# The first MLP's second product by Strassen's scheme with 256 moving columns, and product 3 deferred in the last chunk

## The chip, the core and the metric

The kernel runs on one core of a Trainium2 chip. A core has TensorE (matrix products into PSUM, 8 banks of 128 x 512 fp32), VectorE, ScalarE and GpSimd (POOL), and DMA engines fed by queues, here those of SP and POOL. The engines run side by side and wait for each other by semaphores. The metric is the device time of one execution in microseconds, the median of several.

## The reference

A two-layer encoder on 512 tokens of width 1024, in fp32. Layer 0 mixes by retention (4 heads) and by windowed attention (8 heads), layer 1 by axial-rope attention (8 heads). After each mixer comes an MLP with 4096 features:

```python
x = x + y                                      # y: the mixer's output
h = rms_norm(x, norm_mlp[layer])
x = x + jnp.square(jax.nn.relu(h @ w_mlp_up[layer])) @ w_mlp_down[layer]
```

Here `h` is 512 x 1024, `w_mlp_up` 1024 x 4096 and `w_mlp_down` 4096 x 1024. The text calls `h @ w_mlp_up` the first product and the one with `w_mlp_down` the second.

## The kernel before

**Three matmuls for one.** fp32 operands are split into a high part and a low rest, both of type fp32r (ScalarE casts, VectorE subtracts; `split`, L314 to L321). A product of two tiles is three matmuls, high x high, high x low and low x high (`mm3`, L326, L328, L327). Each has its own 128x128 weight load (PEld).

**Weights.** One stream, `w_stream`, loads 256 x 512 pieces (512 KB) on SP's queue into the blocks of `raws` (L459), and splits each into one of four pairs `wparts` (`cut`, L536 on ScalarE and L538 on VectorE). A piece of the plan is split when a pair comes free, so the splits run at most four pieces ahead of TensorE. `raws` holds 2 blocks until the odd layer's attention is over.

**The order.** All instructions are put in order by a planner written in the kernel: tasks ask for engines, slots and events, costs are estimated (`vec`, `act`, `pe`), and at each step the operation with the earliest estimated start goes next, with a class (EVAC first, then ATT, AUX, LOAD, GEMM) to break ties. The order on each engine is fixed by this; the chip then runs each engine's queue in order.

**First MLP** (`mlp`). Two halves of 2048 features. For each, four column chunks of the first product, then two of the second, all as plain products with the weights stationary and 512 tokens moving, so the result stands transposed (features on partitions). The second product is added to `xT` (L1223), and the next layer's input is formed from each finished tile (`after`: L316, L321).

**Second MLP** (`last_mlp`). Four chunks q of 1024 features. Each takes two column chunks of the first product, 2q and 2q+1, and a second product by Strassen's scheme in Winograd's form: the activations are cut in two token halves and two feature halves, the weights in two feature halves and two column halves (quarters), and 7 products of sums of these stand for 8. The sums of activations are formed by `rest` and `rest2` (L1325), those of weights by `sums` and `t1` (L481, L491, L499, L505; the subtraction of one quarter is done by an accumulating load on POOL's queue, L467). Products 1, 6 and 7 add up in one pair of banks, 5 and 3 in another; `add` takes them from PSUM into `acc_o` (L1398). The order is

```python
PRODUCTS = (2, 1, 4, 6, 5, 7, 3)
...
if pr == 4 and q < 3:
    yield from up(2 * q + 2, ...)      # a chunk of the first product
```

so that in chunks 0 to 2 a chunk of the first product, 96 matmuls, lies between product 4 and product 6, and in the last chunk nothing does. Here the activations are stationary and 512 columns of weights move. The stream has 9 blocks then, and 2 more (`xs`) for sums: five lent by gates and probabilities (`sh0` to `sh4`), the rest by `xT`.

**Axial tables.** `ax_tables` loads the tables for layer 1's rope when retention has ended (L1474, L1479, L307), long before they are read.

Of the kernel before, what the change touches and what calls it, by code (L numbers as in the profile page):

```python
# [17 lines left out]
P = 128  # L18
S = 512
D = 1024  # L20
# [173 lines left out]
FIXED = [0.065, 0.075]  # L194
# [10 lines left out]
def pe(n):  # L205
    return ("P", 3 * (n / 2400 + 0.0135))
# [16 lines left out]
def hybrid_encoder(ctx: ExitStack, tc: tile.TileContext, a, out):  # L223
# [10 lines left out]
    kvp = ctx.enter_context(tc.tile_pool(name="kvp", bufs=4))  # L234
# [5 lines left out]
    FIXED[:] = 0.065, 0.075  # L240
# [10 lines left out]
    raws = slots("raw", 2, (P, 2, 512), F32)  # L251
    wparts = pairs("w", 4, (P, 2, 512))
    bigs = pairs("big", 4, (P, 4, 512))
    def shared(i, dt):
        return cst.tile([P, 2, 512], dt, tag=f"sh{i}", name=f"sh{i}")

    gs = [shared(i, F32) for i in range(2)]
    pts = [shared(i, F32R) for i in range(2, 5)]
    probs_t = Slots(W, [(t[:, 0, :], t[:, 1, :]) for t in pts])
# [3 lines left out]
    xT2 = [cst.tile([P, 2, 512], F32, tag=f"xT{k}", name=f"xT{k}") for k in range(KD // 2)]  # L263
    xT = [xT2[k // 2][:, k % 2, :] for k in range(KD)]
    rB = cst.tile([P, 512], F32, name="rB")

    def kv_pair():
        both = kvp.tile([P, 2, 512], F32R, tag="kv", name="kv")
        return both[:, 0, :], both[:, 1, :]
# [103 lines left out]

    def plan_mlp(l):
        p_ = []
        for hf in range(2):
            for c in range(4):
                p_ += w_parts(f"up{l}", 0, D, hf * 2048 + c * 512)
            for c in range(2):
                p_ += w_parts(f"down{l}", hf * 2048, (hf + 1) * 2048, c * 512)  # L380
        return p_

    plan += plan_mlp(0)
    for c0 in (1024, 0, 512):
        plan += w_parts("w_in_odd", 0, D, c0)
    for r0 in (0, 512):
        for c0 in (0, 512):
            plan += w_parts("w_out_odd", r0, r0 + 512, c0)


    PRODUCTS = (2, 1, 4, 6, 5, 7, 3)
    chunk_at = {}
    loads_of = [ap for _, ap in plan]

    def plan_w(parts):
        plan.extend(parts)
        loads_of.extend(ap for _, ap in parts)

    unit_load = list(range(len(plan)))
    at_product = {}  # L400

    def quarter(q, r, c, h):
        r0 = q * 1024 + (1 - r) * 512 + h * 256
        return a["down1"][r0:r0 + 256, c * 512:c * 512 + 512]

    def plan_up(g, between=()):
        between = list(between)
        for part in w_parts("up1", 0, D, g * 512):
            for at in between[:1]:
                chunk_at[at] = len(loads_of)  # L410
                loads_of.append(quarter(*at))
            del between[:1]
            unit_load.append(len(loads_of))
            plan_w([part])
        for at in between:
            chunk_at[at] = len(loads_of)
            loads_of.append(quarter(*at))

    def plan_products(q, prs):
        for pr in prs:  # L420
            for h in range(2):
                at_product[q, pr, h] = len(plan)
                plan.append((("down1", q, pr, h), None))
                unit_load.append(None)

    plan_up(0)
    for q in range(4):
        plan_up(2 * q + 1, [(q, r, c, h) for r, c in ((0, 1), (0, 0), (1, 0)) for h in range(2)])
        plan_products(q, PRODUCTS[:3])
        last_two = [(q, 1, 1, h) for h in range(2)]  # L430
        if q < 3:
            plan_up(2 * q + 2)
        for at in last_two:
            chunk_at[at] = len(loads_of)
            loads_of.append(quarter(*at))
        plan_products(q, PRODUCTS[3:])

# [121 lines left out]
    def gemm(name, r0, r1, c0, lhs, natural, evac, cls=EVAC, bk=None, halves=False):  # L559
# [6 lines left out]
        for k0 in range(first, nk, step):  # L566
# [6 lines left out]
            for b in range(4):  # L573
                bs = slice(b * P, (b + 1) * P)
                if halves and b == 3:
                    for i, cs in enumerate((slice(0, 256), slice(256, 512))):
                        if k0 == 0:
                            halved.append((yield gbanks))
# [1168 lines left out]
```

## Time and profile before

| | |
|---|---|
| median of 3 runs | 1251.6 us (1251.45 to 1254.9) |
| the profiled execution: time, span | 1252.68 us, 1250.8 us |
| TensorE busy | 1235.5 us, 5736 matmuls |
| VectorE, ScalarE busy | 809.7, 581.5 us |
| mean granted clock of TensorE | 0.997 |
| moved by DMA | 123.52 MB |

The span runs from the first to the last instruction; the time also holds what lies around it. Matmuls overlap, so the length given for one is longer than the distance from its start to the next start.

### The profile page before, as it was taken

Reading aid. Unit: us, or ns where it says so; the run is one execution under the profiler, and the core shown is the slowest. Engines: PE = TensorE matmul, PEld = TensorE weight load, DVE = VectorE, ACT = ScalarE, POOL = GpSimd, SP = SyncE. Lnnn points to the kernel's source line nnn. Section 1 sums busy time; section 2 is a strip of 40 time slices with the busy share of each in tenths; the row PEclk is TensorE's granted clock in tenths of the full one; section 3 lists DMA queues with packets and bytes.
Section 4 is the critical chain, followed back from the end, with each engine's and each line's share of the span. In section 5 each row is a group of like instructions: output and inputs, shape, how many; then the busy total and the mean of one; then the engine's idle time right before and its main releaser. Section 6 shows DMA issues by size and latency. Waiting matters only on the chain.

```text
span 1250.8 us, 15112 instructions
## 1 busy us (share of the span) xinstructions
PE 1235.5 (99%) x5736; PEld 1023.9 (82%) x5736; DVE 809.7 (65%) x1447; ACT 581.5 (46%) x1103; POOL 21.2 (2%) x26
## 2 busy tenths in 40 slices
PE   8999999999999999999999999999999999999997
PEld 6888888888888888888888888778888888888885
DVE  6798578768676452334543268888757768767776
ACT  6687424334445342123433245767465536535352
POOL 0000000000000000000000000000000001001000
PEclk9999999999999999999999999999999999999999
DMA  6521332312233333332322332010553545527421
GB/s 190 175 93 35 86 100 72 96 56 82 67 102 93 101 101 101 101 101 85 95 97 94 101 101 77 26 43 26 187 133 82 139 150 136 135 66 168 151 51 51
DMA packets 68105, 123.52 MB, mean 99 GB/s; under 512 B 5485, under 2 KB 11415, under 8 KB 67776
## 3 DMA queue, kind: packets, MB, share of 16 engines
q1 hardware_dynamic: 63680, 114.16, 28.9%
q0 software_dynamic: 4352, 8.39, 4.3%
q8 instruction: 45, 0.74, 0.2%
q14 instruction: 28, 0.23, 0.1%
HBM read 120.42 MB, written 4.21 MB: 100 GB/s over the span
## 4 chain that ended last, share of the span: by engine, by line
PE 95%; DVE 3%; DMA 1%; issue 0%; ACT 0%; SPq 0%; DVEq 0%
PE bank L326 30%; PE bank L328 30%; PE bank L327 30%; PE bank L332 3%; PE bank L680 1%; DVE wl L538 1%; DVE col L1545 1%; DMA x_nat<-in_x_dram 1%; DVE bigl L319 0%; DVE t L974 0%; SPq L639 0%; DVE xT L1223 0%; PE bank L1260 0%; DVE t L999 0%; DVE bigl L321 0%
## 5 line engine op out<-in xcount | busy, mean ns | idle before, releaser
L538 DVE TENSOR_TENSOR wl<-raw,wh 128x1024 fp32r<-128x1024 f32 x153 | 186.1, 1219 | 170.0 <-ACT wh L536 168.2
L536 ACT CAST wh<-raw 128x1024 fp32r<-128x1024 f32 x153 | 160.4, 1051 | 244.9 <-PE bank L327 191.6
L326 PE MATMUL bank<-hh,wh 128*128 128x512 f32 x512 | 200.7, 392 | 0.0
L328 PE MATMUL bank<-hh,wl 128*128 128x512 f32 x512 | 199.3, 389 | 0.0
L327 PE MATMUL bank<-hl,wh 128*128 128x512 f32 x512 | 199.2, 389 | 0.0
L326 PE MATMUL bank<-bigh,wh 128*128 128x512 f32 x448 | 175.9, 393 | 0.1
L328 PE MATMUL bank<-bigh,wl 128*128 128x512 f32 x448 | 174.6, 390 | 0.0
L327 PE MATMUL bank<-bigl,wh 128*128 128x512 f32 x448 | 174.4, 389 | 0.0
L326 PE MATMUL bank<-wh,hh 128*128 128x512 f32 x368 | 146.9, 399 | 0.0
L328 PE MATMUL bank<-wh,hl 128*128 128x512 f32 x368 | 143.8, 391 | 0.0
L327 PE MATMUL bank<-wl,hh 128*128 128x512 f32 x368 | 143.6, 390 | 0.0
L327 PEld LDWEIGHTS bank<-hl,wh 128*128 128x128 f32 x512 | 96.1, 188 | 20.2 <-issue 0.5
L328 PEld LDWEIGHTS bank<-hh,wl 128*128 128x128 f32 x512 | 96.1, 188 | 20.2
L326 PEld LDWEIGHTS bank<-hh,wh 128*128 128x128 f32 x512 | 96.1, 188 | 20.0 <-issue 0.5
L328 PEld LDWEIGHTS bank<-bigh,wl 128*128 128x128 f32 x448 | 84.1, 188 | 17.7
L326 PEld LDWEIGHTS bank<-bigh,wh 128*128 128x128 f32 x448 | 84.1, 188 | 17.2 <-DVE xT L1223 0.3
L327 PEld LDWEIGHTS bank<-bigl,wh 128*128 128x128 f32 x448 | 84.2, 188 | 17.0
L326 PE MATMUL bank<-wh,bigh 128*128 128x512 f32 x224 | 88.0, 393 | 3.4 <-ACT bigh L314 3.4
L328 PE MATMUL bank<-wh,bigl 128*128 128x512 f32 x224 | 87.8, 392 | 0.2 <-DVE bigl L319 0.2
L327 PE MATMUL bank<-wl,bigh 128*128 128x512 f32 x224 | 87.8, 392 | 0.0
L319 DVE TENSOR_TENSOR bigl<-t,bigh 128x512 fp32r<-128x512 f32 (+1 forms) x112 | 61.8, 573 | 34.4 <-ACT bigh L314 34.4
L328 PEld LDWEIGHTS bank<-wh,hl 128*128 128x128 f32 x368 | 69.2, 188 | 14.8
(200 smaller groups left out, 1851.0 us busy)
## 6 DMA issues: line engine op xcount, KB each, us to landing
raw<-in_w_mlp_up_dram SPq DMA_DIRECT2D x40, 512.0 KB, 3.7
raw<-in_w_mlp_down_dram SPq DMA_DIRECT2D x39, 512.0 KB, 4.1
raw<-in_w_in_even_dram SPq DMA_DIRECT2D x35, 512.0 KB, 4.0
sh<-in_w_mlp_up_dram SPq DMA_DIRECT2D x18, 512.0 KB, 3.7
sh<-in_w_mlp_down_dram SPq DMA_DIRECT2D x17, 512.0 KB, 4.5
raw<-in_w_out_even_dram SPq DMA_DIRECT2D x16, 512.0 KB, 4.2
raw<-in_w_in_odd_dram SPq DMA_DIRECT2D x12, 512.0 KB, 3.7
sh<-in_w_mlp_down_dram POOLq DMA_DIRECT2D x11, 512.0 KB, 5.9
```

The costliest lines, as they stand in the source:

```text
L319: nc.vector.tensor_tensor(out=lo, in0=src, in1=hi.bitcast(F32), op=ALU.subtract)
L326: nc.tensor.matmul(o, lhsT=lh, rhs=rh, start=first, stop=False, **kw)
L327: nc.tensor.matmul(o, lhsT=lh, rhs=rl, start=False, stop=False, **kw)
L328: nc.tensor.matmul(o, lhsT=ll, rhs=rh, start=False, stop=last, **kw)
L332: nc.tensor.transpose(bank[:, j * P:(j + 1) * P], p_, ident)
L536: nc.scalar.copy(out=hi, in_=src)
L538: nc.vector.tensor_tensor(out=lo, in0=src, in1=hi.bitcast(F32), op=ALU.subtract)
L680: nc.tensor.matmul(first_bk[b], lhsT=hs[k][i == 2][:, b * P:(b + 1) * P], rhs=wt, start=k == 0 and i == 0, stop=False)
L1545: nc.vector.reduce_max(out=m, in_=b, axis=mybir.AxisListType.X)
```

## The change

The first MLP is computed as the second: `strassen_mlp` serves both, with two ways to do a product. `add_out` is the second MLP's old way. `add_part` is for the first MLP, whose result has to stand transposed: the weights are stationary and the 256 tokens of a half move, so that a matmul is 128x256 and a bank holds two blocks of columns side by side. A product is then 48 matmuls in place of 24 of 128x512, each with its weight load.

`mlp_steps` writes the order for both MLPs: product 3 of the third chunk is taken out of it and put between product 4 and product 6 of the last chunk. Weight pairs are given back after each half product, not after both halves.

The first MLP's stream gets nine more blocks when retention has ended, the five of gates and probabilities and the four of keys and values (`blocks_to_weights`). When product 4 of its last chunk has been placed, `ax_blocks` takes seven back for the odd layer's keys, values and probabilities, and `ax_tables`, which moves there, gets the two blocks for sums. Outside the MLPs the planner's fixed cost of a matmul falls from 0.0135 to 0.0025 us, and the squares for the norm go from class EVAC to AUX. Not shown: the lent blocks' bookkeeping (`block`, `anew`), `plan_quarter`, `add_out`, and the removal of the old functions and of the unused `halves` branch in `gemm`.

```diff
-FIXED = [0.065, 0.075]
+FIXED = [0.065, 0.075, 0.0025]
...
-    return ("P", 3 * (n / 2400 + 0.0135))
+    return ("P", 3 * (n / 2400 + FIXED[2]))
...
+    def mlp_steps(l):
+        steps = [("up", 8 * l)]
+        for q in range(4 * l, 4 * l + 4):
+            end = q % 4 == 3
+            steps += [("up", 2 * q + 1), (q, 2), (q, 1), (q, 4)]
+            steps += [(q - 1, 3)] if end else [("up", 2 * q + 2)]
+            steps += [(q, 6), (q, 5), (q, 7)] + ([] if q % 4 == 2 else [(q, 3)])
+        return steps
...
+        for q, n in mlp_steps(l):
...
+                    plan_quarter(*at)
+            else:
+                for h in range(2):
+                    at_product[q, n, h] = len(plan)
+                    plan.append((("down", q, n, h), None))
+                    unit_load.append(None)
+                    if (n == 6 and q % 4 != 2) or (n == 7 and q % 4 == 2):
+                        plan_quarter(q, 1, 1, h)
+    plan_mlp(0)
...
-            W.spawn(square(k), EVAC)
+            W.spawn(square(k), AUX)
...
+        def part(q, name, i, cs):
+            _, ub, got, _ = state[q]
+            if name not in got:
+                got[name] = W.event()
+                ub[name] = yield bigs
+                got[name].set()
+            yield got[name]
+            return ub[name][0][:, i, cs], ub[name][1][:, i, cs]
...
+        def sums(q, i, t_, f):
+            ev = state[q][0]
+            c = yield temps
+            yield ev["A", i]
+            yield from minus(c[:, half[0]], t_[:, half[1]], f[:, half[1]], ALU.add)
+            yield from minus(c[:, half[1]], c[:, half[0]], t_[:, half[0]])
+            hi, lo = yield from part(q, "C", i, slice(0, 512))
+            yield from split(hi, lo, c, 512)
+            ev["1", i].set()
+            W.spawn(sums2(q, i, t_, f, c), AUX)
...
+            hi, lo = yield from part(q, "D", i, half[0])
+            yield from split(hi, lo, f[:, half[0]], 256)
+            ev["D", i].set()
+            temps.give(f)
+        of = {1: ("A", "A", 0, "X", True, ((0, 0),)), 2: ("B", "B", 0, "Y", True, ((0, 0),)),
+              4: ("B", "B", 1, "V", True, ((1, 0),)), 6: ("C", "1", 1, "X", False, ((0, 1),)),
+              5: ("C", "1", 0, "Z", True, ((1, 1),)), 7: ("A", "3", 1, "X", False, ((1, 0), (1, 1))),
+              3: ("D", "D", 0, "Z", False, ((0, 1),))}
+        open_, read = {}, {}
...
+        for q, n in mlp_steps(l):
+            if q == "up":
+                yield from gemm(f"up{l}", 0, D, n % 8 * 512, lambda k: (h_ev[k], hs[k]), False, up_evac(n // 2, n % 2))
+                continue
+            name, evn, hf, bn, opens, outs = of[n]
+            ev, ub, _, _ = state[q]
+            for h in range(2):
+                w = w_used[0]
+                assert plan[w][0] == ("down", q, n, h), (plan[w][0], q, n, h)
+                yield w_ready[w]
+                for b in range(2):
+                    if h == 0:
+                        if opens:
+                            open_[q, bn, b] = yield gbanks
+                        else:
+                            yield read[q, bn, b]
+                    yield from product(open_[q, bn, b], b, 2 * h, [ev[evn, i] for i in range(NT)], ub[name], hf * 256, w_tiles[w], opens)
+                    if h == 1:
+                        read[q, bn, b] = W.spawn(product.add(b, open_[q, bn, b], outs, n in (2, 4, 7, 3), q % 4 == 3 and n in (1, 3, 7)), EVAC)
+                wparts.give(w_tiles[w])
+                w_used[0] += 1
+            for n_ in {7: "A", 5: "C", 3: "D", 4: "B"}.get(n, ""):
+                bigs.give(ub[n_])
+            if (q, n) == (3, 4):
+                W.spawn(ax_tables(), LOAD)
+                W.spawn(ax_blocks(), EVAC)
+        gbanks.left -= 2
+        FIXED[:] = 0.065, 0.075, 0.0025
...
+    def add_part(after):
+        left = [2] * NT
+        def add(b, bank, outs, closes, final):
+            for r, c in outs:
+                j = 2 * c + b
+                o = xT2[j][:, :, r * 256:(r + 1) * 256]
+                yield vec(512)
+                nc.vector.tensor_tensor(out=o, in0=bank.rearrange("p (k n) -> p k n", k=2), in1=o, op=ALU.add)
+                if closes and (r, c) == outs[-1]:
                     gbanks.give(bank)
...
+                    left[j] -= 1
+                    if not left[j]:
+                        for k in range(2):
+                            yield from after(2 * j + k)
+        def product(bank, b, i0, ev, u, u0, w, opens):
+            for k in range(2):
+                bs = slice((2 * b + k) * P, (2 * b + k + 1) * P)
+                for ii in range(2):
+                    i = i0 + ii
+                    yield ev[i]
+                    yield pe(256)
+                    mm3(bank[:, k * 256:(k + 1) * 256], (w[0][:, ii, bs], w[1][:, ii, bs]),
+                        (u[0][:, i, u0:u0 + 256], u[1][:, i, u0:u0 + 256]),
+                        opens and i == 0 and k == 0, i == NT - 1 and k == 1, skip_group_check=not opens)
+        product.add = add
+        return product
...
+    def blocks_to_weights():
+        probs_t.free.clear()
+        gates.free.clear()
+        for i in range(5):
+            raws.add(block(f"sh{i}"))
+        for i in range(4):
+            (raws if i < 2 else xs).add(block(f"kv{i}"))
...
+    def ax_blocks():
+        for _ in range(4):
+            ax["kv"].append(anew((yield raws), F32R))
+        kA.extend(both(t) for t in ax["kv"][:2])
+        vA.extend(both(t) for t in ax["kv"][2:])
+        ax_kv.set()
+        for _ in range(3):
+            t = anew((yield raws), F32R)
+            ax["p"].append(t)
+            probs_t.add(both(t))
...
                            in_=a["c_ax"][:, i * P:(i + 1) * P].rearrange("(t p) d -> p t d", p=P))
         yield Sleep(W.now + 4.0)
         for i in range(4):
-            axt.append((yield gates))
+            axt.append(ax["t"][i // 2][:, i % 2, :])
...
         W.spawn(norm_rows(counted, box, rB0), EVAC)
-        W.spawn(ax_tables(ret1), AUX)
+        blocks_to_weights()
...
-        yield from mlp(0, hn_ready, rB0, None, after)
+        yield from strassen_mlp(0, hn_ready, rB0, add_part(after))
...
+        yield from strassen_mlp(1, hn_ready, rB1, add_out())
```

## Rows read from the trace of the kernel before

**Rows 1.** The page, part 1: busy us, share of the span, instructions.

```profile
PE 1235.5 (99%) x5736; PEld 1023.9 (82%) x5736; DVE 809.7 (65%) x1447; ACT 581.5 (46%) x1103; POOL 21.2 (2%) x26
```

**Rows 2.** The page, part 4: the chain that ended last, by engine.

```profile
PE 95%; DVE 3%; DMA 1%; issue 0%; ACT 0%; SPq 0%; DVEq 0%
```

**Rows 3.** Windows: stretch, its length, busy us (instructions) of each engine, clock, DMA.

```profile
380.62:729.68 349.06, 349.06 (x1539) 288.67 (x1538) 142.97 (x164) 118.17 (x149) 0.00 (x0) 1.00 0.31 97
729.68:909.10 179.42, 176.39 (x849) 144.62 (x848) 142.85 (x356) 109.25 (x279) 1.34 (x1) 0.99 0.24 76
930.00:1210.00 280.00, 280.00 (x1237) 231.81 (x1236) 204.46 (x291) 137.68 (x187) 15.83 (x13) 1.00 0.44 120
1210.00:1250.00 40.00, 32.50 (x134) 25.77 (x132) 28.04 (x46) 12.52 (x19) 1.22 (x1) 0.96 0.25 71
```

**Rows 4.** Groups by line and form, TensorE, 380.62 to 729.6.

```profile
L326 PE MATMUL bank<-hh,wh 128*128 128x512 f32 x256 | 100.0, 391 | 0.0
...
L326 PE MATMUL bank<-bigh,wh 128*128 128x512 f32 x256 | 99.6, 389 | 0.0
```

**Rows 5.** The chain in order of time, from 380: start, us, what.

```profile
386.90 0.86 PE bank L1260 x2
```

**Rows 6.** Timeline from 231: start us, us, engine, line, operation, output<-inputs.

```profile
231.06 0.28 PE L326 MATMUL bank<-kv,sh 128*128 128x256 f32 x1
231.06 0.19 PEld L327 LDWEIGHTS bank<-kv,sh 128*128 128x128 f32 x1
...
233.81 0.28 PE L328 MATMUL bank<-kv,sh 128*128 128x256 f32 x1
...
233.93 0.39 PE L326 MATMUL bank<-bigh,bigh 128*128 128x512 f32 x1
```

**Rows 7.** Timeline of TensorE from 1221 to 1231; in brackets idle before, releaser.

```profile
1221.56 0.39 PE L328 MATMUL bank<-wh,bigl 128*128 128x512 f32 x1
1225.32 0.50 PE L326 MATMUL bank<-wh,bigh 128*128 128x512 f32 x1 [3.37 <-ACT bigh L314]
...
1226.27 0.54 PE L328 MATMUL bank<-wh,bigl 128*128 128x512 f32 x1 [0.23 <-DVE bigl L319]
1226.61 0.63 PE L326 MATMUL bank<-wh,bigh 128*128 128x512 f32 x1
...
1230.02 0.40 PE L328 MATMUL bank<-wh,bigl 128*128 128x512 f32 x1
```

**Rows 8.** Timeline of ScalarE and of VectorE, the same stretch.

```profile
1224.64 1.54 ACT L314 CAST bigh<-t 128x512 fp32r<-128x512 f32 x4 [1.68 <-DVE t L1325]
...
1225.54 1.02 DVE L319 TENSOR_TENSOR bigl<-t,bigh 128x512 fp32r<-128x512 f32 x2
```

**Rows 9.** Groups by line and form, VectorE, 930 to 1210: busy, mean ns.

```profile
L538 DVE TENSOR_TENSOR wl<-sh,wh 128x1024 fp32r<-128x1024 f32 x34 | 41.4, 1221 | 28.8 <-ACT wh L536 28.5
L1398 DVE TENSOR_TENSOR acc_o<-bank,acc_o 128x512 f32<-128x512 f32 x50 | 32.9, 684 | 1.8 <-PE bank L328 1.3
```

**Rows 10.** Timeline of SP's queue from 350: first and last of the table loads.

```profile
351.74 0.46 SPq L1474 DMA_DIRECT2D t<-in_ax_q_norm_dram  x1
...
358.23 0.93 SPq L307 DMA_DIRECT2D t<-in_c_ax_dram  x2
```

**Rows 11.** Groups by line and form, VectorE, 381 to 730.

```profile
L321 DVE SCALAR_TENSOR_TENSOR hl<-xT,cols,hh 128x512 fp32r<-128x512 f32 x9 | 6.7, 749 | 0.2 <-ACT hh L316 0.2
```

**Rows 12.** Timeline of SP's queue, 1160 to 1182: the last chunk's loads, first and last.

```profile
1160.60 0.37 SPq L459 DMA_DIRECT2D raw<-in_w_mlp_up_dram  x1
...
1180.12 0.37 SPq L459 DMA_DIRECT2D sh<-in_w_mlp_down_dram  x1
```

**Rows 13.** Timeline of TensorE from 1197: the last chunk's first product begins.

```profile
1202.06 0.39 PE L326 MATMUL bank<-wh,bigh 128*128 128x512 f32 x1
```

More of the change, by code (lines that the diff above doesn't have):

```diff
@@ L372, in hybrid_encoder, with plan_w @@
             plan += w_parts("w_out_even", r0, r0 + 512, c0)
-    def plan_mlp(l):
[L375 to L383, printed above, removed]
+    chunk_at, at_product = {}, {}
+    loads_of = [ap for _, ap in plan]
+    unit_load = list(range(len(plan)))
+    def plan_w(parts):
+        for part in parts:
+            unit_load.append(len(loads_of))
+            plan.append(part)
+            loads_of.append(part[1])
@@ L402, in quarter @@
[L402 to L417, printed above, removed]
@@ new lines, in evac @@
+                name, cs = ("A", half[0]) if second else ("B", slice(0, 512))
+                if second:
+                    W.spawn(sums(q, i, t_, first[i]), ATT)
+                else:
+                    first[i] = t_
+                hi, lo = yield from part(q, name, i, cs)
+                yield from split(hi, lo, t_[:, cs], cs.stop)
+                ev[name, i].set()
+            return evac
+        def sums(q, i, t_, f):
[8 more added lines that the diff above has]
+            W.spawn(sums2(q, i, t_, f, c), AUX)
@@ new lines, in add_out, with add, product @@
+    def add_out():
+        def add(b, bank, outs, closes, final):
+            for r, c in outs:
+                t = 2 * r + b
+                o = acc_o[t, c]
+                yield acc_ready[t, c]
+                yield vec(512)
+                nc.vector.tensor_tensor(out=o, in0=bank, in1=o, op=ALU.add)
+                if closes and (r, c) == outs[-1]:
+                    gbanks.give(bank)
+                if final:
+                    yield ("D", 0.8)
+                    nc.sync.dma_start(out=out[0, t * P:(t + 1) * P, c * 512:(c + 1) * 512], in_=o)
+        def product(bank, b, i0, ev, u, u0, w, opens):
+            us = slice(u0 + b * P, u0 + (b + 1) * P)
+            for ii in range(2):
+                i = i0 + ii
+                yield ev[i]
+                yield pe(512)
+                mm3(bank, (u[0][:, i, us], u[1][:, i, us]), (w[0][:, ii, :], w[1][:, ii, :]),
+                    opens and i == 0, i == NT - 1, skip_group_check=not opens)
+        product.add = add
+        return product
@@ L1465, in hybrid_encoder, with blocks_to_weights2, ax_tables @@
+    def blocks_to_weights2(done):
+        probs_t.free.clear()
+        for t in ax["p"] + ax["t"]:
+            raws.add(anew(t))
+        for e in done:
+            yield e
+        for k in range(KD // 2):
+            (raws if k < 2 else xs).add(anew(xT2[k]))
     axt, axt_ready = [], W.event()
-    def ax_tables(after):
-        yield after
+    def ax_tables():
+        for _ in range(2):
+            ax["t"].append(anew((yield xs)))
         gn = yield temps
@@ L1499, in evac_kv_ax @@
         yield axt_ready
-        if not kA:
-            kA.extend(kv_pair() for _ in range(2))
-            vA.extend(kv_pair() for _ in range(2))
+        yield ax_kv
         nat = yield temps
```

270 lines of the change are left out of this document (68 added, 202 removed), and 3 rows, old and new, of the table of.

## The prediction

> **What bounds the kernel now.** I read the page first, for the engines' shares. TensorE is busy 1235.5 of 1250.8 us, VectorE 809.7 and ScalarE 581.5 [rows 1], and the chain that ended last is TensorE for 95% [rows 2]. So time can be won only by giving TensorE less work or by closing its holes, and vector work costs nothing as long as TensorE does not wait for it. Second, the table of windows, to see which stage has holes [rows 3]. The first MLP has none: 349.06 us busy in 349.06. The odd layer's attention stage (729.68 to 909.10) is busy 176.39 of 179.42 with a granted clock of 0.99. The second MLP, which already uses the seven products, is busy 280 of 280 us up to 1210, with VectorE at 204.46 (73%) and ScalarE at 137.68 (49%); in the 40 us after that TensorE is idle for 7.5, about 4 of them behind its last matmul, and the granted clock falls to 0.96. Third, the groups by line and form inside the first MLP, to count matmuls [rows 4], and the chain there, for the one piece of work that is no product, 0.86 us of norm [rows 5]. Last, the timeline of the one stretch of 256-column matmuls [rows 6] and of the hole near the end [rows 7, 8].
>
> **Pace of the old form.** The first MLP has 256 x 3 matmuls of the first product and 256 x 3 of the second [rows 4], 1536 in all. (349.06 - 0.86) / 1536 = 0.2267 us from start to start. The 389 ns in those rows is the length of one, overlapped with the next, and is not the pace. The second product thus costs 768 x 0.2267 = 174.1 us.
>
> **Part 1: seven products with 256 moving columns.** For each of the 4 feature chunks there are 7 products; a product is 2 row halves x 2 banks x 2 column blocks x 2 contraction tiles x 3 = 48 matmuls of 128x256. That is 4 x 7 x 48 = 1344, and a weight load goes with each. Counted in columns it is 7/8 of the old work. If a half-width matmul took half of 0.2267, the sum would be 152.3 us, a gain of 21.8; this is the low bound. The nearest row is the retention stage: 24 matmuls of 128x256 in a row, each with its own 128x128 load, start between 231.06 and 233.93 [rows 6], 0.1196 us each. The high bound is the 0.19 us that a weight load shows as its length there: 1344 x 0.19 = 255.4, a loss of 81.3. I take the row that is the same form with the same load: 1344 x 0.1196 = 160.7. **Term: 160.7 - 174.1 = -13.4 us.** About 0.013 us per matmul that does not shrink with its width, paid 576 times more often, eats 8.4 of the 21.8. As the row is read to 0.01 us in 2.87, the term is good to about 1.5 us.
>
> Against this stands a rule. The Trainium skill, "TensorE: Matmul & The Clock Gate", Part 3: Packing small matmuls, says that a weight load overlaps matmuls in flight only where it goes to other rows of the array; loads of all 128 rows, as here, would then lie bare. Bare loads are rival D below; the row disagrees, since 24 such pairs at 0.1196 us leave no room for a bare load of 0.19 [rows 6].
>
> **Part 2: the vector work of the scheme.** The first MLP gets what the second has: sums of four blocks of the activations and their splits, sums of the weight quarters, 24 more weight splits at 1.22 us and 48 more additions at 0.68 [rows 9]. The second MLP's window gives the price as a whole: 204.46 us of VectorE in 280 is 243 us over 332 us; with the norm and the next layer's input about 258 of 336, 77%, and ScalarE some 53% [rows 3]. In the second MLP just this lies hidden behind TensorE for 280 us on end, with each product at 5.44 us (24 x 0.2267); here a product lasts 5.74 (48 x 0.1196), so it has more cover, not less. **Term: 0**; uncovered it costs holes as in part 4 (rival C).
>
> **Part 3: buffers and queues.** The weight stream gets nine lent blocks (five of gates and probabilities, four of keys and values) beside the two it has, which makes nine for loads and two for sums, as in the second MLP. They come free when retention ends, before the last output projection, and no other reader is left. The 16 accumulating loads from the POOL queue become 32; POOL is 2% busy [rows 1]. At the end of the first MLP the blocks go back: seven of them are taken as the last products' weights are split, so about two are left for the next layer's weights, as before. The axial tables move there: 10 small loads and 2 larger ones, from 351.74 to 359.16 on SP, 7.4 us in which no weight load can be issued behind them [rows 10]. They start when 28.7 us of products are still ahead (five of 5.74) and the first reader comes some 14 us later still. **Term: 0**; without that cover up to 7.4.
>
> The next layer's input is now late by more. Product 7 closes one half of the result and product 3 the other. Behind product 3 come an addition (0.68) and two splits in turn (VectorE's part 0.75 each [rows 11]) for each bank, some 4.5 us by ScalarE and VectorE together; the second half of the input is first read 48 matmuls, 10.9 us, into the next projection, so it is hidden. For the first half product 3 itself is the cover, 5.74 us against about 5. That is tight. **Term: +0.8, from 0 to 6.**
>
> **Part 4: product 3 deferred, both MLPs.** Now, in the last chunk, product 6 follows product 4 with no first-product chunk between. The timeline shows the matmul at 1221.56 followed at 1225.32, released by ScalarE's split of the last sum (the casts from 1224.64), then waiting for VectorE's low part at 1226.27 [rows 7, 8]. The eight from 1226.61 to 1230.02 start 0.43 us apart, at the lower clock of 1.2 GHz, after TensorE had stood idle. From 1221.56 to 1230.02 twelve matmuls start: 12 x 0.2267 = 2.72 of 8.46 us, so the hole costs 5.74, of which about 1.6 is the clock. The change puts product 3 of the chunk before there: 24 matmuls, 5.44 us. The first need moves from 1221.79 to 1227.23, the operands were there at 1225.32 and 1226.27. What comes in ahead of them is two additions (1.37 us); the two extra weight splits are paced by TensorE's release of their buffers and move with it. Margin 1.0 less at most 1.4, so about closed. **Term: -5.2**, from -5.7 (all) to -1.5 (two splits of 1.22 us each come in front too, and part of the low clock stays).
>
> The price is that two weight blocks are held for a third of a chunk longer. The last chunk's loads are issued from 1160.60 to 1180.12 and its products begin at 1202.06 [rows 12, 13]: 20 us of slack. Nothing.
>
> **Part 5: the order written elsewhere.** The planner's cost for a matmul falls outside the MLPs and the squares for the norm get a lower class. No instruction is added; engine orders in both attention stages may move. The odd one loses 3.0 us to idling and about 1.8 to the clock [rows 3]. **Term: 0, within 3 either way.**
>
> **Sum.** 1252.68 (the profiled execution, 1.9 us more than its span) - 13.4 - 5.2 + 0.8 = 1234.9. The median of the three runs is 1.1 below the profiled one: **1233.8 us**, 1.4% less.
>
> **Rivals.**
> A (forecast): both gains come. 1229 to 1238, chance 0.70.
> B: one hole of the size seen stays or opens anew, where the last chunk's sums are still late or at the handover to the odd layer. For it: the margin of part 4 is within its error. Against: the moved work is paced by TensorE. 1251.6 - 13.4 + 0.8 = 1239.0, with a second hole 1244.8. Chance 0.16.
> B': the new orders also close part of the attention's 4.8 us: 1225 to 1229. Chance 0.04.
> C, on the other side: VectorE can't keep up in the first MLP, and each of its four chunks opens a hole like the one in [rows 7] between product 4 and product 6. The price is 5.74 each, 23 in all: 1256.8. From three holes on (17.8 / 5.74) the whole gain is gone. For it: VectorE goes from 143 to about 258 us there. Against: 280 us of the second MLP with the same work and no idle TensorE [rows 3]. Chance 0.08, of which 0.04 slower, 0.03 no change.
> D: weight loads aren't hidden behind 256 columns; every matmul costs at least the load's 0.19. 1251.6 + 81.3 - 5.2 + 0.8 = 1328.5. It decides from 0.1335 us a matmul ((174.1 + 5.2) / 1344). For it only the recorded length of a load, against it the 24 starts. Chance 0.02.
>
> **How the numbers follow.** A measurement of this kernel tells about 0.3% (3.8 us) from no change. Faster is A, B, B' and the rest of C, 0.91; within 0.3% 0.03; slower 0.06. From 1228.5 to 1242 lie A almost whole and most of B; the bounds of parts 3 to 5 (up 5.2, 3.7 and 3, down 0.8, 0.5 and 3) are taken in as they would seldom add up.
>
> **What would show it.** The matmuls should be 6312 instead of 5736; those of 128x256 in the first MLP should start 0.119 to 0.121 us apart; from the first MLP's first matmul to the next projection some 336 us instead of 349; no idle TensorE of 3 us and no half clock between product 4 and product 6 of either last chunk; the POOL queue with 32 accumulating loads. I am wrong if the start-to-start distance is above 0.125, if the first MLP shows idle TensorE behind VectorE's sums, or if the next layer's projection starts late.

## The result, and the profile after

The changed kernel takes 1235.41 us (median of 4 runs, 1233.98 to 1237.72) beside 1251.53 us of the kernel before (4 runs, 1251.0 to 1254.9) on the same chip: a ratio of 0.9867, 95% interval 0.9844 to 0.989. The forecast was 1233.8 us, from 1228.5 to 1242. The profiled execution is the longest of the four: 1237.72 us, span 1235.8.

The page of the kernel after, parts 1 and 4 and one line of part 3 (queue, kind: packets, MB, share), answers to [rows 1] and [rows 2]:

```profile
PE 1223.5 (99%) x6312; PEld 1041.5 (84%) x6312; DVE 923.9 (75%) x1649; ACT 631.2 (51%) x1189; POOL 40.7 (3%) x42
...
q0 software_dynamic: 8704, 16.78, 8.3%
...
PE 97%; DVE 1%; DMA 1%; ACT 0%; issue 0%; SPq 0%; ACTq 0%; DVEq 0%
```

There are 6312 matmuls, as counted ahead, TensorE is busy 12.0 us less, and VectorE works 114 us more. The windows of the kernel after, by stage, answer to [rows 3] (the stages are even layer, first MLP, odd layer, second MLP):

```profile
26.29:382.72 356.43, 356.43 (x1784) 300.66 (x1783) 263.61 (x553) 176.46 (x417) 1.33 (x1) 1.00 0.32 99
382.72:721.87 339.15, 337.16 (x2116) 305.97 (x2114) 251.35 (x356) 166.04 (x228) 18.28 (x15) 1.00 0.42 115
721.87:898.00 176.13, 174.71 (x850) 143.19 (x849) 149.56 (x369) 110.09 (x284) 1.21 (x1) 1.00 0.25 78
898.00:1235.80 337.80, 332.06 (x1475) 273.38 (x1473) 243.90 (x350) 163.61 (x227) 18.26 (x15) 1.00 0.43 116
```

A stage runs from the first matmul of its first product to that of the next, the last one to the span's end. By the same cut in both traces:

| stage (us) | before | after | difference | forecast |
|---|---|---|---|---|
| opening | 22.70 | 26.29 | +3.59 | 0 |
| even layer | 357.92 | 356.43 | -1.49 | 0 |
| first MLP | 349.06 | 339.15 | -9.91 | -13.4 |
| odd layer, with its handover | 179.42 | 176.13 | -3.29 | +0.8 |
| second MLP | 341.70 | 337.80 | -3.90 | -5.2 |

The opening's +3.59 isn't put down to the change: nothing in the diff touches its instructions, and in the profiles of the experiments below, which share them, it took 22.3 to 25.1 us. (Its matmuls run slower in this execution: four from 11.31 take 2.05 us, where four from 11.38 in the kernel before take 1.17.) So the stages are compared one by one from here on.

**The pace.** The groups by line and form, TensorE, over the first MLP of the kernel after, answer to [rows 4]:

```profile
L344 PE MATMUL bank<-bigl,wh 128*128 128x256 f32 x448 | 127.0, 283 | 0.9 <-DVE bigl L336 0.9
L343 PE MATMUL bank<-bigh,wh 128*128 128x256 f32 x448 | 126.8, 283 | 1.1 <-ACT bigh L331 1.1
L345 PE MATMUL bank<-bigh,wl 128*128 128x256 f32 x448 | 126.8, 283 | 0.0
```

3 x 448 is the 1344 of part 1, and two of the three groups have a wait in front that the first MLP didn't have before. The timeline of TensorE at the handover shows the pace, which answers to [rows 6]:

```profile
721.03 0.28 PE L345 MATMUL bank<-bigh,wl 128*128 128x256 f32 x1
...
721.75 0.28 PE L345 MATMUL bank<-bigh,wl 128*128 128x256 f32 x1
721.87 0.40 PE L343 MATMUL bank<-wh,hh 128*128 128x512 f32 x1
```

0.12 us from start to start. So the second product takes 1344 x 0.12 = 161.3 us, and the first MLP without a hole would take 0.86 + 174.1 + 161.3 = 336.3. It takes 339.15.

**The holes.** The timeline of TensorE in the last chunk of the first MLP, at the second half of product 7:

```profile
710.95 0.28 PE L345 MATMUL bank<-bigh,wl 128*128 128x256 f32 x1
712.29 0.38 PE L343 MATMUL bank<-bigh,wh 128*128 128x256 f32 x1 [1.06 <-ACT bigh L331]
713.61 0.39 PE L344 MATMUL bank<-bigl,wh 128*128 128x256 f32 x1 [0.94 <-DVE bigl L336]
713.83 0.28 PE L345 MATMUL bank<-bigh,wl 128*128 128x256 f32 x1
713.95 0.28 PE L343 MATMUL bank<-bigh,wh 128*128 128x256 f32 x1
```

From 710.95 to 713.95 four matmuls start in place of 3.00 / 0.12 = 25: 2.5 us lost. Product 7's operand is the second set of sums (`sums2`), and it is formed just in time or later. In the second MLP's last chunk the first set, product 6's operand, still comes late (this answers to [rows 7]):

```profile
1210.47 0.39 PE L345 MATMUL bank<-wh,bigl 128*128 128x512 f32 x1
1212.18 0.50 PE L343 MATMUL bank<-wh,bigh 128*128 128x512 f32 x1 [1.33 <-ACT bigh L331]
1212.52 0.40 PE L344 MATMUL bank<-wl,bigh 128*128 128x512 f32 x1
1213.22 0.50 PE L345 MATMUL bank<-wh,bigl 128*128 128x512 f32 x1 [0.30 <-DVE bigl L336]
...
1214.04 0.40 PE L345 MATMUL bank<-wh,bigl 128*128 128x512 f32 x1
```

Six matmuls from 1210.47 to 1214.04, 3.57 us, are worth 6 x 0.2267 = 1.36; 2.2 us are lost where 5.74 were before, and TensorE doesn't fall to the lower clock behind it: the starts after 1213.22 stand 0.23 to 0.34 apart, at a granted clock of 1.00.

The waiting matmul is the sixteenth of product 6, the first that reads its fourth block of activations: 87 matmuls of 0.2267 us lie between 1202.06 [rows 13] and the hole before, 72 of them products 2, 1 and 4. The operand slid back with the product put in front of it. Before, this matmul started 3.76 us after the one ahead of it (1225.32 after 1221.56 [rows 7]), now 1.71 (1212.18 after 1210.47), but product 3's 24 matmuls, 5.44 us, come before it as well: counted from product 4 it starts 1.71 + 5.44 - 3.76 = 3.4 us later than before. So the wait is shorter by 2.0 us alone (1.33 after 3.37); the rest of the gain is the low clock, which is gone.

**Why the operands are late.** Windows of the kernel after: chunk 0 of the first MLP from product 2 to product 6, then the last chunk of the first MLP from product 3 into product 7, and that of the second MLP from product 2 into product 6:

```profile
426.30:465.60 39.30, 39.30 (x243) 35.50 (x242) 30.82 (x52) 23.60 (x36) 4.88 (x4) 1.00 0.56 134
690.50:714.00 23.50, 21.51 (x175) 20.91 (x174) 21.63 (x35) 11.24 (x17) 0.00 (x0) 1.00 0.20 57
1185.10:1213.00 27.90, 26.49 (x116) 21.30 (x114) 24.91 (x36) 16.95 (x22) 2.42 (x2) 1.00 0.33 76
```

VectorE is busy 78% in the first, 92% and 89% in the two others. Its mean over the whole first MLP is 251.35 of 339.15, 74%, and says nothing about these places.

### The profile page after: what moved, and what is told of

It reads as the page before. It is cut to its first block, busy times and chain, and to the rows that moved or that the text cites. A ratio compares the mean times of both kernels' runs of the same rounds, so it can differ in the third digit from the quotient of the medians.

```text
span 1235.8 us, 16617 instructions
## 1 busy us (share of the span) xinstructions
PE 1223.5 (99%) x6312; PEld 1041.5 (84%) x6312; DVE 923.9 (75%) x1649; ACT 631.2 (51%) x1189; POOL 40.7 (3%) x42
## 3 DMA queue, kind: packets, MB, share of 16 engines
q0 software_dynamic: 8704, 16.78, 8.3%
## 4 chain that ended last, share of the span: by engine, by line
PE 97%; DVE 1%; DMA 1%; ACT 0%; issue 0%; SPq 0%; ACTq 0%; DVEq 0%
PE bank L343 31%; PE bank L345 31%; PE bank L344 31%; PE bank L349 4%; PE bank L674 1%; DMA x_nat<-in_x_dram 1%; DVE wl L548 0%; DVE t L1235 0%; DMA kv<-in_w_in_odd_dram 0%; ACT wh L546 0%; SPq L633 0%; DVE hl L338 0%; PE bank L1254 0%; DVE bigl L336 0%; DVE xT L1409 0%
## 5 line engine op out<-in xcount | busy, mean ns | idle before, releaser
L343 PE MATMUL bank<-bigh,wh 128*128 128x256 f32 (+1 forms) x640 | 203.3, 318 | 1.1 <-ACT bigh L331 1.1
L344 PE MATMUL bank<-bigl,wh 128*128 128x256 f32 (+1 forms) x640 | 201.9, 315 | 0.9 <-DVE bigl L336 0.9
L345 PE MATMUL bank<-bigh,wl 128*128 128x256 f32 (+1 forms) x640 | 201.8, 315 | 0.0
L546 ACT CAST wh<-sh 128x1024 fp32r<-128x1024 f32 x82 | 86.0, 1048 | 80.9 <-PE bank L344 52.1
L548 DVE TENSOR_TENSOR wl<-sh,wh 128x1024 fp32r<-128x1024 f32 x82 | 100.3, 1223 | 28.4 <-ACT wh L546 27.4
L548 DVE TENSOR_TENSOR wl<-kv,wh 128x1024 fp32r<-128x1024 f32 x71 | 86.4, 1223 | 37.0 <-ACT wh L546 35.2
L546 ACT CAST wh<-raw 128x1024 fp32r<-128x1024 f32 x68 | 71.1, 1049 | 75.7 <-PE bank L344 41.6
L546 ACT CAST wh<-kv 128x1024 fp32r<-128x1024 f32 x71 | 74.0, 1048 | 69.0 <-PE bank L344 45.5
L548 DVE TENSOR_TENSOR wl<-raw,wh 128x1024 fp32r<-128x1024 f32 x68 | 82.5, 1216 | 34.8 <-ACT wh L546 34.2
L336 DVE TENSOR_TENSOR bigl<-t,bigh 128x256 fp32r<-128x256 f32 (+1 forms) x160 | 79.6, 526 | 19.4 <-ACT bigh L331 19.4
```

The lines of the kernel that those rows point to most:

```text
L336: nc.vector.tensor_tensor(out=lo, in0=src, in1=hi.bitcast(F32), op=ALU.subtract)
L343: nc.tensor.matmul(o, lhsT=lh, rhs=rh, start=first, stop=False, **kw)
L344: nc.tensor.matmul(o, lhsT=lh, rhs=rl, start=False, stop=False, **kw)
L345: nc.tensor.matmul(o, lhsT=ll, rhs=rh, start=False, stop=last, **kw)
L546: nc.scalar.copy(out=hi, in_=src)
L548: nc.vector.tensor_tensor(out=lo, in0=src, in1=hi.bitcast(F32), op=ALU.subtract)
```

## Experiments

All compare with the kernel before on the same chip, and the stages come from one profile of each. The first theory: the gain is the 256-column products and the deferred product, each at about its forecast price, less the holes shown; the order elsewhere (part 5) gives nothing. The rivals: the deferral gives nothing, or part of the gain comes from the planner's costs.

**Product 3 in its own chunk, in both MLPs, and in the second alone.**

```diff
-            steps += [(q - 1, 3)] if end else [("up", 2 * q + 2)]
-            steps += [(q, 6), (q, 5), (q, 7)] + ([] if q % 4 == 2 else [(q, 3)])
+            steps += [] if end else [("up", 2 * q + 2)]
+            steps += [(q, 6), (q, 5), (q, 7), (q, 3)]
```

(For the second alone, `end and l` stands in place of `end` in the first line, and the rest as it was for the first MLP.)

> The changed kernel with product 3 left in its own chunk in both MLPs. Theory (the deferral covers late sums): the second MLP loses again about 5.7 us behind product 4 of its last chunk where the changed kernel loses 1.9, and the first MLP opens a hole there too, 3 to 5 us for the 2.9 it has now: 1240 to 1243 us against 1235.4, with a row of idle TensorE over 3 us in each last chunk. Rival (the deferral only moves the hole, the second MLP's gain came from elsewhere): within 2 us of 1235.4.

> The deferral kept in the first MLP and undone in the second. Theory: only the second MLP's hole comes back, 3.8 us: 1239. Rival (nothing from the deferral): 1235.4. The difference to the kernel without any deferral is what the first MLP's deferral is worth; the theory says 1 to 4 us.

Measured: 1242.04 us (ratio to the kernel before 0.9916, 95% interval 0.9901 to 0.993) and 1237.88 us (0.9882, 0.9865 to 0.9898). In the second case the second MLP takes 342.0 us in place of 337.8, and the timeline of TensorE has the old hole back at the same place:

```profile
1210.03 0.79 PE L343 MATMUL bank<-wh,bigh 128*128 128x512 f32 x1 [3.38 <-ACT bigh L331]
```

By this profile the deferral is worth 4.2 us there; the kernel without any deferral has 341.1 in its second MLP, which gives 3.3. In the first MLP it is worth 341.47 - 339.15 = 2.3 us, and 1.7 in the odd layer (177.65 beside 175.92), at whose start TensorE waits 1.8 us for the input's low part without it and 1.1 with it.

**The planner's old costs; the matmul cost alone.** The first kernel undoes both edits of part 5, the second only the first.

```diff
-FIXED = [0.065, 0.075, 0.0025]
+FIXED = [0.065, 0.075, 0.0135]
...
-            W.spawn(square(k), AUX)
+            W.spawn(square(k), EVAC)
```

> The changed kernel with the planner's old cost of a matmul outside the MLPs and the squares in their old class. Theory (these two moved the orders, and the odd layer's stage went from 179.4 to 176.1 us and the even one from 357.9 to 356.4 by them): about 1240 us, the odd stage near 179. Rival (that is only chance of one execution, or came from other edits such as the tables' new place): 1235.4, the odd stage near 176.

> The changed kernel with the planner's old cost of a matmul outside the MLPs, and the squares left in their new class. Theory (the matmul's cost is what moved the odd stage): the odd stage near 182 as with both undone, 1241. Rival (the class of the squares did it): the odd stage stays at 176, 1236.

Measured: 1242.14 us (0.9911, 0.9896 to 0.9926) and 1239.58 us (0.9898, 0.9885 to 0.9911). The odd layer takes 182.03 and 181.11 us in place of 176.13; the second MLP is the same (337.76 in both). The timelines of TensorE in the attention stage show where. First the kernel before, then the one with the old matmul cost alone:

```profile
784.84 0.50 PE L326 MATMUL bank<-kv,bigh 128*128 128x512 f32 x1 [1.28 <-ACT t L1550]
786.36 0.79 PE L326 MATMUL bank<-kv,bigh 128*128 128x512 f32 x1 [0.55 <-DVE bigl L319]
844.47 0.66 PE L332 MATMUL bank<-ident,t 128*128 128x128 f32 x4 [1.04 <-ACT t L1550]
```

```profile
776.07 0.50 PE L343 MATMUL bank<-sh,bigh 128*128 128x512 f32 x1 [1.38 <-ACT t L1578]
777.59 0.80 PE L343 MATMUL bank<-sh,bigh 128*128 128x512 f32 x1 [0.55 <-DVE bigl L336]
835.56 0.66 PE L349 MATMUL bank<-ident,t 128*128 128x128 f32 x4 [1.15 <-ACT t L1578]
```

They are the same three waits in the same order; the window 760 to 790 of the kernel before has a granted clock of 0.94. The changed kernel has none of them, and 1.00 throughout. With the lower cost the planner writes another order, and the waits are gone: 5.0 us by stages (181.11 - 176.13), 4.2 by the medians. The class of the squares is worth the rest, 1.5 us in the first MLP and 0.9 in the odd layer. The three waits sum to 3.1 us, and the window 752 to 782 of the kernel with the old cost, which holds the first two, has a granted clock of 0.94. The even layer gets 0.6 (357.06 beside 356.43). Part 5's term of 0 falls.

**512 moving columns in the first MLP's products.** The half-width is there because the result has to stand transposed. This kernel does the first MLP's products as 24 matmuls of 128x512 with the activations stationary; it leaves out the transposed result that the next layer needs (the sums are added untransposed), all other work is unchanged.

```diff
-            for k in range(2):
-                bs = slice((2 * b + k) * P, (2 * b + k + 1) * P)
+            us = slice(u0 + b * P, u0 + (b + 1) * P)
...
-                    yield pe(256)
-                    mm3(bank[:, k * 256:(k + 1) * 256], (w[0][:, ii, bs], w[1][:, ii, bs]),
-                        (u[0][:, i, u0:u0 + 256], u[1][:, i, u0:u0 + 256]),
+                yield pe(512)
+                mm3(bank, (u[0][:, i, us], u[1][:, i, us]), (w[0][:, ii, :], w[1][:, ii, :]),
```

> The first MLP's products by 24 matmuls of 128x512 with the activations stationary in place of 48 of 128x256; its result is then added untransposed, so the output is not the reference's. All else alike. Theory (a fixed 0.013 us per matmul is what the half width costs): 672 x 0.2267 = 152.3 us of products for 161.3: 1226.4, -9.0. Rival (vector work or loads hold the first MLP as soon as TensorE is faster): between 1229 and 1235, with new idle TensorE behind ScalarE or VectorE in the first MLP.

Measured: 1228.21 us (0.9805, 0.9791 to 0.982); first MLP 333.34 us, 5.8 less. The pace alone gives 161.3 - 672 x 0.2267 = 9.0. The missing 3.2 are lost in the last chunk: with 0.30 us less cover per product, product 6 and product 7 both wait there (timeline of TensorE), and behind the first wait the granted clock is 0.62 from 689.49 to 694.00, where matmuls start 0.43 us apart:

```profile
689.49 0.50 PE L343 MATMUL bank<-wh,bigh 128*128 128x512 f32 x1 [1.33 <-ACT bigh L331]
...
703.94 0.50 PE L343 MATMUL bank<-wh,bigh 128*128 128x512 f32 x1 [1.11 <-ACT bigh L331]
```

The width's price is thus as part 1 has it, and in the last chunk TensorE loses a third of what it wins.

**Vector work added to the first MLP.** For each block of activations one subtraction is repeated 8 times, then, in a second kernel, 2 times; the values don't change. The expectations count 11.6 and 2.9 us of VectorE more in each of the four chunks, at 0.36 us an operation; in the first MLP's windows VectorE is busy 293.59 and 261.12 us in place of 251.35, so it is 10.6 and 2.4.

```diff
             yield from minus(c[:, half[1]], c[:, half[0]], t_[:, half[0]])
+            for _ in range(8 if l == 0 else 0):
+                yield from minus(c[:, half[1]], c[:, half[0]], t_[:, half[0]])
```

> The changed kernel with one subtraction of the sums repeated eight times more for each of the 16 tiles of the first MLP: 128 operations of about 0.36 us, some 46 us more of VectorE, from 74% to about 88% of that stage. Theory (vector work has room behind TensorE there): the first MLP's stage grows by less than 6 us, and only in the last chunk, where there is no other cover. Rival (VectorE is at its limit): it grows by 20 us or more, with idle TensorE in every chunk.

> The changed kernel with one subtraction repeated twice more, in place of eight times, for each tile of the first MLP: 32 operations, some 11 us of VectorE, 2.9 us per chunk. Eight more were 11.6 us per chunk, and cost 44 us in holes of product 6 in all four chunks; between the first product's chunk and product 6 VectorE has 8.5 us of 39.3 free in the first chunk. Theory (the cover there is those 8 us): under 3 us more in the first MLP, in the last chunk alone. Rival (there is no free time, every added operation is paid): 8 to 11 us, in all four chunks.

Measured: 1279.11 us (1.021, 1.0194 to 1.0226) and 1237.54 us (0.9882, 0.9868 to 0.9896); first MLP 383.27 and 343.07 us in place of 339.15. With 10.6 us more, product 6 of each of the four chunks waits; the first (timeline of TensorE; a window of 39.30 us from product 2 to product 6 of chunk 0, as for the changed kernel above; and the window around the wait):

```profile
471.49 0.58 PE L343 MATMUL bank<-bigh,wh 128*128 128x256 f32 x1 [5.81 <-ACT bigh L331]
472.94 0.58 PE L344 MATMUL bank<-bigl,wh 128*128 128x256 f32 x1 [0.87 <-DVE bigl L336]
```

```profile
422.39:461.69 39.30, 39.30 (x243) 35.51 (x242) 35.81 (x69) 20.94 (x27) 4.88 (x4) 1.00 0.58 134
465.68:475.00 9.32, 2.65 (x11) 2.35 (x11) 7.54 (x14) 3.92 (x8) 0.00 (x0) 0.66 0.40 129
```

With 2.4 us more only the last chunk does:

```profile
700.03 0.39 PE L343 MATMUL bank<-bigh,wh 128*128 128x256 f32 x1 [4.29 <-ACT bigh L331]
700.99 0.58 PE L344 MATMUL bank<-bigl,wh 128*128 128x256 f32 x1 [0.57 <-DVE bigl L336]
```

I was far off with the first, which I had costed at less than 6 us by the mean share. Chunks 0 to 2 have 39.30 - 30.82 = 8.5 us of idle VectorE ahead of product 6, but not all of it can be used: with 10.6 us more, where the operand comes late, VectorE is still idle for 39.30 - 35.81 = 3.5 us of the same stretch. 2.4 more cost nothing there, 10.6 cost 6.7 us of wait and a granted clock of 0.66 around it. The margin is thus some 4 to 5 us (10.6 - 6.7 = 3.9; 8.5 - 3.5 = 5.0). The last chunk has nothing to spare: 2.4 more cost 3.9. Rival C's mechanism is real; the first three chunks are some 4 to 5 us of VectorE away from it, the last one is in it.

**Moving the sums.** If VectorE's order is at fault, one of these should close the holes. A: one more scratch tile of 128x512 (12), so that the last set of sums needn't wait for one. B: due times of the additions and subtractions of both sets 1.5 us earlier, and the second set in class EVAC. C: A, and product 7's operand ahead of the rest of its set in every chunk, due 1.0 us earlier in the last chunks. D: A, and the earlier due time alone.

```diff
-        temps = slots("t", 11, (P, 512), F32)
+        temps = slots("t", 12, (P, 512), F32)
...
-            yield vec(256)
+            yield vec(256) + (lambda: -1.5,)
...
-            W.spawn(sums2(q, i, t_, f, c), AUX)
+            W.spawn(sums2(q, i, t_, f, c), EVAC)
...
+            soon = ((lambda: -1.0),) if q % 4 == 3 else ()
+            yield vec(256) + soon
```

(The first edit is A's, the next two B's, the last C's and D's.)

> The changed kernel with 12 in place of 11 scratch tiles for the sums of activations. Each of the four tiles of a chunk holds three of them (two squares and the sum) until its second set of sums is formed, so the fourth sum waits for the first to be given back. Theory B (the holes left, 2.9 us in the first MLP and 1.9 in the second, come from this shortage): the second MLP's stage falls from 337.8 towards 335.9, the first from 339.2 towards 336.5; 1231 to 1233. Theory O (the order in the queues: the sums stand behind weight splits that TensorE paces): no change by more than 1 us.

> The changed kernel with the sums of activations put ahead of other vector work by the planner (an earlier due time of 1.5 us, and the second set of sums in the highest class). Theory O (the holes come from sums and splits that stand behind weight splits paced by TensorE): holes of both last chunks gone, 1231 to 1233. Theory B (scratch tiles): the second set is formed earlier, which gives the tiles back earlier too, so the second MLP's hole goes as well, but the first MLP's hole in product 7 is not one of tiles and stays.

> 12 scratch tiles, and in the last chunk of each MLP the operand of product 7 (the first half of the second set of sums) is formed and split ahead of product 3's and due 1.0 us earlier to the planner. Theory (after the scratch tile, the hole in product 7 is what is left, 2.0 us in the second MLP and 2.0 with its low clock's tail in the first, and it is one of order): both holes gone, first MLP near 336.5, second near 335.6: about 1230 to 1231. Rival (VectorE is simply full in the last chunk): the hole moves to product 3 or back to product 6 and the time stays at 1234.

> 12 scratch tiles, and only the due time of product 7's operand moved 1.0 us earlier in the last chunks, with the order inside the sums as it was. Theory as before, with less room, since product 3's sum still stands in between: 1230 to 1233. Rival: 1234, the hole elsewhere.

| kernel | us | ratio, interval | first MLP | second MLP |
|---|---|---|---|---|
| A | 1234.02 | 0.9856, 0.9843 to 0.987 | 339.11 | 337.62 |
| B | 1252.69 | 1.0001, 0.9991 to 1.0011 | 341.81 | 353.79 |
| C | 1241.77 | 0.9905, 0.9889 to 0.9922 | 342.27 | 340.97 |
| D | 1236.75 | 0.9879, 0.9865 to 0.9893 | 341.61 | 337.59 |

None wins anything that this measures. In A product 6 of the second MLP no longer waits, but product 7 does; in C product 6 does again (timelines of TensorE, A and then C):

```profile
1220.13 0.50 PE L345 MATMUL bank<-wh,bigl 128*128 128x512 f32 x1 [1.98 <-DVE bigl L336]
```

```profile
1214.55 0.50 PE L345 MATMUL bank<-wh,bigl 128*128 128x512 f32 x1 [2.59 <-DVE bigl L336]
1216.39 0.52 PE L345 MATMUL bank<-wh,bigl 128*128 128x512 f32 x1 [0.88 <-DVE bigl L336]
```

In B product 1 waits in all four chunks of the second MLP (0.77 and 0.97 us each time), and product 6 in the last chunk of both MLPs (3.0 and 2.5 us). So another order on VectorE moves the hole and doesn't close it, as far as these four show.

**The second set's subtractions on GpSimd.** A, and in the last chunk of each MLP the two subtractions of `sums2` per block go to GpSimd: eight operations of 128x256 for each MLP.

```diff
-            yield from minus(t_[:, half[0]], t_[:, half[0]], t_[:, half[1]])
-            yield from minus(f[:, half[0]], f[:, half[0]], c[:, half[1]])
+            if q % 4 == 3:
+                for o, x, y in ((t_, t_[:, half[0]], t_[:, half[1]]), (f, f[:, half[0]], c[:, half[1]])):
+                    nc.gpsimd.tensor_tensor(out=o[:, half[0]], in0=x, in1=y, op=ALU.subtract)
+                    yield Sleep(W.now + 0.7)
+            else:
...
```

> The changed kernel with twelve scratch tiles of 256 columns, and in the last chunk of each MLP the two subtractions per quarter that make product 7's operand are done by GpSimd in place of VectorE (eight operations per MLP, about 2.9 us less of VectorE in each last chunk). Theory (VectorE is full in the last chunks, 89 to 92% there, so that work taken off it closes the hole and work only moved in order doesn't): first MLP 336.5 to 338 us in place of 339.1, second MLP about 336 in place of 337.6, total 1230 to 1232. Rival (the operations take longer on GpSimd than the late sums can bear, or slow VectorE beside them): the operand of product 7 comes later than now, a hole of 1 us or more ahead of product 7 in each MLP stays or grows, total 1234 to 1238.

Measured: 1229.86 us (1229.31 to 1230.16; 0.9823, 0.981 to 0.9836). First MLP 336.38 us, where 336.3 was worked out for no hole, second MLP 336.09. (The expectation's "256 columns" for the scratch tiles should read 512.) The waits of TensorE (us in total, times, longest) in this kernel:

```profile
PE bank L345 <- DVE hl L338: 1.6, 2, 1.3
...
PE bank L345 <- DVE bigl L336: 0.5, 1, 0.5
```

Those of the changed kernel:

```profile
PE bank L343 <- ACT bigh L331: 2.4, 2, 1.3
...
PE bank L345 <- DVE hl L338: 1.3, 2, 1.0
...
PE bank L344 <- DVE bigl L336: 0.9, 1, 0.9
PE bank L345 <- DVE bigl L336: 0.3, 1, 0.3
```

Of the 3.6 us that TensorE waits for sums there, 0.5 is left; the wait of 1.6 is the handover's.

The numbers came as the theory had them, but not for the reason that it gives. The timelines of GpSimd and of VectorE in the first MLP's last chunk:

```profile
679.97 1.24 POOL L1353 TENSOR_TENSOR t<-t 128x256 f32<-128x256 f32 x1
...
683.44 1.23 POOL L1353 TENSOR_TENSOR t<-t,t 128x256 f32<-128x256 f32 x1
...
680.69 0.69 DVE L1414 TENSOR_TENSOR xT<-bank,xT 128x512 f32<-128x512 f32 x1
681.65 4.11 DVE L548 TENSOR_TENSOR wl<-sh,wh 128x1024 fp32r<-128x1024 f32 x1 [0.27 <-ACT wh L546]
```

A weight split that takes 1.22 us elsewhere takes 4.11 while six subtractions run on GpSimd: 2.9 us given back, about what eight subtractions take. So VectorE isn't relieved; in the 23.5 us that answer to the window 690.50 to 714.00 above it is busy 23.50. What differs is the time: GpSimd's queue is empty, and the eight subtractions are over by 688.5; in the changed kernel, whose first MLP starts 4 us later, those on VectorE stood between weight splits and additions, from 691.10 to 710.59, the last one over at 711.01 and product 7 late at 712.29. The stall on VectorE (681.65 to 685.76) falls where TensorE waits for nothing, and the old place had no slack. This is a reading of one pair of traces: that the earlier start closes the hole, and not another part of the new order, is not shown. Whether relief without that stall would give more was not tried, nor this edit together with 512 moving columns.

## Why the prediction was right, point by point

**Part 1** (-13.4): right in mechanism and nearly in size. Start to start is 0.12 us where 0.1196 was read, 161.3 us for 1344 matmuls, -12.8. By the rule of the Trainium skill that the prediction weighed ("TensorE: Matmul & The Clock Gate", Part 3: Packing small matmuls) 0.19 us of load would lie bare in each (rival D); 1344 loads lie hidden in the pace shown, so the measurement decides for the row of the retention stage.

**Part 2** (0): the term failed by 2.5 to 2.9 us, in the first MLP's last chunk. Its reason, a mean share of 77% (74% measured) and 5.74 us of cover per product, holds for chunks 0 to 2, where the added vector work shows the margin. It doesn't hold where no chunk of the first product stands between product 4 and product 6. The 280 us of the second MLP that it took as proof end at 1210, before product 6 of its last chunk. One of its signs of being wrong, idle TensorE behind the sums in the first MLP, is there (1.06 and 0.94 us).

**Part 3** (+0.8): at the handover TensorE waits 1.3 us (0.28 and 1.02, for the low part of the input on VectorE), inside the range of 0 to 6; the tables and lent blocks show no wait of TensorE. The 32 accumulating loads are there: 16.78 MB on POOL's queue at 0.52 MB each.

**Part 4** (-5.2): measured -4.2 by the kernel without the deferral in the second MLP, -3.3 by the one without any, -3.9 between the traces, and inside -5.7 to -1.5. The hole that it reads as one between product 4 and product 6 lies inside product 6; its sum uses the distances alone and stands. The half clock is gone, the waits are down from about 3.6 to 1.6 us. The step that was mis-sized is "margin 1.0 less at most 1.4, so about closed": the operand slid by 3.4 us, where two additions (1.37) were allowed. The two weight splits that the term left out and its lower bound counted (2 x 1.22) would make 3.8, and they are there: from product 4's end to the late operand VectorE does two splits in the kernel before (1219.67, 1222.38) and four in the changed one (1203.14, 1205.86, 1208.62, 1211.34). Pacing by TensorE brings them into the stretch, it doesn't keep them out.

**Part 5** (0, within 3): the step that failed. The lower matmul cost gives 5.0 us in the odd layer, by the three waits that it removes, and the squares' class some 2.4 more. The odd layer's gain of 3.3 is these 5.9 there (182.03 - 176.13) less 2.6 that the rest of the change costs (182.03 with both edits undone, beside 179.42 before). This is what rival B' describes, at a chance of 0.04 by itself; it came together with the small holes of B, and the two nearly cancel. Of the even layer's 1.5 the lower cost explains 0.6; the cause of the rest stays open.

**The sum.** First MLP +3.5, second +1.3, odd layer -4.1 and even layer -1.5 against the forecast give -0.8; with the opening's +3.6 the profiled execution stands 2.8 above its forecast of 1234.9, and the median 1.6 above 1233.8. The total was right partly by luck: two errors of about 5 us have opposite signs, the MLPs' holes and the order elsewhere. With part 5's two edits undone the rest of the change gives 1252.89 - 1242.14 = 10.8 us, where 17.8 were forecast for it.

## What to carry to other kernels

A helper engine's mean share over a stage doesn't say what it can still take: look at the shortest stretch between the event that frees its work and the first reader, and count idle time there (8.5 us in one chunk, 1.9 in the last). Even that is a bound from above: about half of the 8.5 could be used. Where that is full, reordering on the same engine moved the hole in all four trials; an idle engine's queue started the work earlier, though it gave no relief in sum. And a change of a planner's cost "elsewhere" is a change of the order: give it its own term, and undo it by itself.

## What was not expected of the hardware

GpSimd's work holds VectorE up. While six 128x256 subtractions ran on GpSimd (starts 0.70 us apart, each 1.2 long; one on VectorE takes 0.42), a VectorE operation of 1.22 us took 4.11, and in the second MLP an operation of 0.42 among the sums took 4.13 (start 1190.73). The addition at 680.69, one of whose inputs is a PSUM bank, ran beside them in its usual 0.69. The Trainium skill, "SBUF — State Buffer", Who interferes with whom, says that a VectorE instruction with two inputs in SBUF contends with a GpSimd instruction that reads SBUF, and that one with at most one such input doesn't, outside the two-port modes; these rows agree. In these rows the wait lasts over several GpSimd operations in a row.

An idle TensorE costs more than its wait, and the half clock costs a 128x256 matmul less than double. With 10.6 us of vector work more per chunk the first MLP lost 44.1 us, and its waits there sum to 32.2 (24.2 and 8.0 in the table of waits). Behind the first of them, after TensorE had stood idle for 5.81 and 0.87 us, the granted clock is 0.50 from 473.32 to 477.80, the lower level of 1.2 GHz, and the matmuls there start 0.213 us apart, 1.78 times the 0.12 at 2.4 GHz.
